# A fused encoder layer on one core: the first level of a gated scan, its parity sums moved behind its scalings

## The chip, the cores and the metric

The kernel is one program on one core of a Trainium2 chip. A core has TensorE (PE in the profile, with its weight loads as PEld), VectorE (DVE), ScalarE (ACT), GpSimd (POOL) and SyncE (SP, which only issues transfers). The profile gives each engine's instructions and what each of them waited for. The metric is the device time of one execution in microseconds (us), the median of several; less is better.

## The reference, cut to what matters

One layer over 512 tokens of width 1024, batch 1: token mixing (rotary attention with 8 query and 2 key heads of 64, beside a bidirectional gated scan, HGRN2, with 4 heads of 128 x 128), attention into 256 memory tokens, and a gated MLP with a convolution. The change lies in the gated scan:

```python
def bidirectional_gated_scan(q, logf_fwd, logf_bwd, v):
    ...
    ks = -jnp.expm1(lf)
    ...
    def step(S, xs):
        qx, kx, vx, lx = xs
        bcum = jnp.cumsum(lx, axis=-2)
        diff = bcum[..., :, None, :] - bcum[..., None, :, :]
        dec = jnp.exp(jnp.where(tri, diff, -jnp.inf))
        a = jnp.einsum("...tk,...sk,...tsk->...ts", qx, kx, dec)
        o_intra = jnp.einsum("...ts,...sv->...tv", a, vx)
        o_inter = jnp.einsum("...tk,...kv->...tv", qx * jnp.exp(bcum), S)
        ...
    return out[0] + flip(out[1])
```

For each pair of positions t and s, query and key are multiplied, weighted by all forget gates between them, and summed over the 128 channels; the two directions are added.

## The kernel before, in words

**The scan without steps.** The kernel has no loop over time. For each head, `hgrn_core(h)` builds the 512 x 512 weights between positions by levels m = 1, 2, 4, ... 256: pairs of positions whose blocks of m are neighbours are handled together. `qk` holds queries and keys of both directions with channels on the partitions and time along the row (128 x 2048); `tt` holds the products of the gates over blocks. A level does four things. ScalarE copies the keys in the level's order into a small buffer `kc` (L653). TensorE multiplies them with the queries, four matmuls of 128x128 in float32 (L656). VectorE scales both halves of `qk` by the gates (two operations of 128x512, L682), so that the next level finds them weighted, and multiplies the gates in pairs (L687). VectorE takes the level's pairs from the sums over into `diag` (L689). For m = 128 the matmuls are L663 and go to the other half of the weights; for m = 256 the keys are transposed (L668) and multiplied with the values to the state (L673, copied in L675).

**Ahead of the levels** stand the sums of position t with itself and with its neighbour (`near`, 128 x 1024: elementwise products in L634 to L639). They are split into a high part (a cast on ScalarE, L122) and a rest (a subtraction on VectorE, L123), each 128x1024, and summed over the channels by four matmuls of 128x512 against a pattern of ones and zeros, `parity` (L646); ScalarE copies the result to `diag` (L647). Behind the levels, L696 to L698 multiply the weights and the state with the values; ScalarE squares (L702), GpSimd takes the root (L297, L298), VectorE scales by root and gate (L708), TensorE turns the result (L712).

**The order.** Three cores (h = 0, 1, 2) are woven with the projections: `weave` takes the stream that is least far on by the numbers that each `yield` hands it, against totals of 100 for the projections and 53 (`CORE_SHARE`) for the cores. The first yield of a core is `PREP`. The framework then sets the final order on each engine, which is shown below. The fourth core is woven with the attention (`attention`: scores L883, turns L893) and with the projection of the memory's keys and values (L279 to L281 into `ps_b`, 128x256, results split by L122 and L123); the attention's own keys are turned there too (`turn_k`, L768, behind the second and the third projection of the memory). Other lines that come up: L318 turns the normalised memory rows, L279 to L281 are the three matmuls of every projection (high x high, high x low, low x high), L738 to L761 are the norm and rotation of the attention's queries and keys, L791 turns the queries, L223, L225 and L230 split the weights.

**Buffers.** Small buffers of 128x512 float32 come from rings: tag `th` has four, tag `ta` four, tag `tq` three; `tmp4` (128x1024) has two. A bank of the accumulators (`ps_s`, `ps_o`, `ps_c`, `ps_b`) has two per tag.

## Time and profile before

| | us |
|---|---|
| median of 3 runs | 817.83 (817.6 to 818.08) |
| the profiled execution | 818.56 |
| its span, first to last instruction | 816.8 |
| TensorE busy | 802.4 (98%) |
| VectorE busy | 583.4 (71%) |
| ScalarE busy | 481.7 (59%) |
| GpSimd busy | 137.2 (17%) |
| mean granted TensorE clock | 0.998 |

The span is from the first to the last instruction; what the profiled execution takes beyond it lies ahead of and behind the program. Rows of the timeline read: start, length (us), engine, line, operation, out<-in, shape, count, and in brackets the idle time before and what ended it. Rows of waits read: engine, what it was about to write, its line, what it waited for, total, times, longest (us). The weave of the three cores lies at 54 to 198 us, the fourth core with the attention behind it.

### The profile page before, as it was taken

What the parts mean: (1) busy time and instruction counts of PE and PEld (TensorE: products, weight loads), DVE (VectorE), ACT (ScalarE), POOL (GpSimd) and SP (SyncE); (2) the same over time, 40 slices, a digit from 0 to 9 for tenths busy, and PEclk for the clock granted to TensorE, in tenths of its full rate; (3) what the DMA queues carried; (4) which work ended last, traced back from release to release, by engine and by line L of the source; (5) the groups of instructions that cost most, each with busy time, mean ns of one, the idle gap of its engine ahead of it and who ended that gap; (6) DMA issues with size and microseconds to landing.
All of it is one profiled execution on the core that took longest, in us unless ns stands there. A gap on an engine that the chain in (4) does not pass through costs nothing.

```text
span 816.8 us, 11680 instructions
## 1 busy us (share of the span) xinstructions
PE 802.4 (98%) x4378; PEld 687.1 (84%) x4378; DVE 583.4 (71%) x875; ACT 481.7 (59%) x793; POOL 137.2 (17%) x215
## 2 busy tenths in 40 slices
PE   9999998999999999999999999999999999999996
PEld 7888877889898887888888898899999998888885
DVE  5476597659987774865453767987777788888765
ACT  5675756458988874644552543565555544566651
POOL 0111201044233201301010321211111101000301
PEclk9999999999999999999999999999999999999999
DMA  8596653558998844256734048676766577268852
GB/s 301 186 261 149 154 126 81 126 131 225 279 269 210 201 130 168 76 181 145 192 116 142 27 160 206 141 206 169 192 164 161 129 202 183 91 206 272 244 128 103
DMA packets 42458, 139.54 MB, mean 171 GB/s; under 512 B 5281, under 2 KB 6561, under 8 KB 42401
## 3 DMA queue, kind: packets, MB, share of 16 engines
q1 hardware_dynamic: 28944, 97.37, 34.9%
q0 software_dynamic: 12160, 38.54, 26.3%
q10 hardware_dynamic: 1296, 2.89, 1.0%
q8 instruction: 34, 0.56, 0.3%
q14 instruction: 24, 0.19, 0.1%
HBM read 135.11 MB, written 25.17 MB: 196 GB/s over the span
## 4 chain that ended last, share of the span: by engine, by line
PE 88%; DVE 6%; ACT 2%; DMA 2%; issue 1%; POOL 0%; DVEq 0%; POOLq 0%; SPq 0%
PE ps_b L280 9%; PE ps_b L281 9%; PE ps_b L279 9%; PE ps_s L281 6%; PE ps_s L280 6%; PE ps_s L279 6%; PE ps_o L279 5%; PE ps_o L281 5%; PE ps_o L280 5%; PE ps_c L279 5%; PE ps_c L280 5%; PE ps_c L281 5%; PE ps_c L656 3%; PE ps_o L904 2%; DMA raw<-in_w_dram 2%; PE ps_s L883 2%
## 5 line engine op out<-in xcount | busy, mean ns | idle before, releaser
L223 ACT CAST wh<-raw 128x1024 fp32r<-128x1024 f32 x110 | 113.7, 1035 | 106.8 <-PE ps_b L280 27.8
L225 DVE TENSOR_TENSOR wl<-raw,wh 128x1024 fp32r<-128x1024 f32 (+1 forms) x77 | 92.2, 1199 | 72.3 <-ACT wh L223 72.2
L279 PE MATMUL ps_b<-big,wh 128*128 128x512 f32 (+1 forms) x344 | 122.2, 355 | 0.0
L281 PE MATMUL ps_b<-big,wl 128*128 128x512 f32 (+1 forms) x344 | 120.9, 352 | 0.0
L280 PE MATMUL ps_b<-big,wh 128*128 128x512 f32 (+1 forms) x344 | 120.7, 351 | 0.0
L281 PEld LDWEIGHTS ps_b<-big,wl 128*128 128x128 f32 x344 | 65.0, 189 | 8.5 <-DMA wl<-in_wu_dram 0.2
L279 PEld LDWEIGHTS ps_b<-big,wh 128*128 128x128 f32 x344 | 65.1, 189 | 8.2
L280 PEld LDWEIGHTS ps_b<-big,wh 128*128 128x128 f32 x344 | 65.1, 189 | 8.2
L682 DVE TENSOR_TENSOR big<-big 128x512 f32<-128x512 f32 x64 | 48.1, 761 | 10.4 <-PE ps_c L656 6.2
L279 PE MATMUL ps_s<-wh,big 128*128 128x512 f32 (+1 forms) x140 | 53.2, 381 | 0.9 <-DVE big L123 0.9
L280 PE MATMUL ps_s<-wl,big 128*128 128x512 f32 (+1 forms) x140 | 53.2, 380 | 0.0
L281 PE MATMUL ps_s<-wh,big 128*128 128x512 f32 (+1 forms) x140 | 52.8, 377 | 0.0
L231 POOL DMA_DIRECT2D wl<-in_w_dram x33 | 29.5, 894 | 119.4 <-ACT wl L230 94.9
L123 DVE TENSOR_TENSOR big<-ps_o,big 128x512 fp32r<-128x512 f32 x54 | 36.9, 686 | 12.2 <-ACT big L122 11.9
L122 ACT CAST big<-ps_o 128x512 fp32r<-128x512 f32 x54 | 31.7, 589 | 16.1 <-PE ps_o L1007 7.5
L279 PE MATMUL ps_s<-big,wh 128*128 128x256 f32 (+1 forms) x120 | 40.0, 333 | 0.0
L280 PE MATMUL ps_s<-big,wh 128*128 128x256 f32 (+1 forms) x120 | 39.9, 333 | 0.0
L281 PE MATMUL ps_s<-big,wl 128*128 128x256 f32 (+1 forms) x120 | 39.9, 332 | 0.0
L280 PE MATMUL ps_c<-big,wh 128*128 128x256 f32 (+1 forms) x120 | 39.1, 326 | 0.0
L279 PE MATMUL ps_c<-big,wh 128*128 128x256 f32 (+1 forms) x120 | 39.1, 325 | 0.0
L281 PE MATMUL ps_c<-big,wl 128*128 128x256 f32 (+1 forms) x120 | 39.0, 325 | 0.0
L279 PE MATMUL ps_o<-wh,big 128*128 128x512 f32 (+1 forms) x102 | 38.9, 381 | 0.0
(316 smaller groups left out, 2150.4 us busy)
## 6 DMA issues: line engine op xcount, KB each, us to landing
raw<-in_w_dram SPq DMA_DIRECT2D x91, 512.0 KB, 3.5
wl<-in_w_dram POOLq DMA_DIRECT2D x33, 512.0 KB, 7.5
sum_t<-in_wd_dram SPq DMA_DIRECT2D x20, 512.0 KB, 6.1
tmp<-in_wu_dram SPq DMA_DIRECT2D x14, 512.0 KB, 8.0
sum_t<-in_wd_dram POOLq DMA_DIRECT2D x10, 512.0 KB, 8.3
sum_t<-sum_t POOLq DMA_DIRECT2D x10, 512.0 KB, 7.9
big<-sum_t SPq DMA_DIRECT2D x10, 512.0 KB, 4.5
raw<-sum_t SPq DMA_DIRECT2D x10, 512.0 KB, 3.9
```

The lines of the kernel that those rows point to most:

```text
L122: nc.scalar.copy(hi, src)
L123: (eng or nc.vector).tensor_sub(lo, src, hi.bitcast(F32))
L223: nc.scalar.copy(wh, raw)
L225: last_low[0] = nc.vector.tensor_sub(wl[:, :by_dma], raw[:, :by_dma], wh[:, :by_dma].bitcast(F32)).ins
L231: nc.gpsimd.dma_start(wl[:, by_dma:], source(i)[:, by_dma:], accum_op=ALU.add)
L279: nc.tensor.matmul(o, a[0], b[0], start=start, stop=False, skip_group_check=again)
L280: nc.tensor.matmul(o, a[0], b[1], start=False, stop=False, skip_group_check=again)
L281: last_mm[0] = nc.tensor.matmul(o, a[1], b[0], start=False, stop=stop, skip_group_check=again).ins
L656: nc.tensor.matmul(o[:, b, :], kc[:, blk(b)], pat(qk, b * P, [[2 * m, P // (2 * m)], [T + m, 2], [1, m]]), start=True, stop=True)
L682: nc.vector.tensor_tensor(out=c, in0=c, in1=pat(tt, toff + off, [[2, npair], [gap, 2], [0, m]]), op=ALU.mult)
L883: nc.tensor.matmul(s, qT[h // 4][:, h % 4, blk(qb)], kT[:, 2 * (h // 4) + c, :], start=c == 0, stop=c == 1)
L904: nc.tensor.matmul(o, vv[:, c, h // 4].rearrange("p a d -> p (a d)"), pt[j][:, c, :], start=c + j == 0, stop=c == 3 and j == 1)
```

## The change

Three edits. In `hgrn_core` the products `near` are no longer split in two operations into two `tmp4` buffers, but by halves: two casts and two subtractions of 128x512 into four buffers of the ring `th`, which the sum of the keys and the level copies use too. The four sums and the copy into `diag` move from ahead of the levels into level m = 1, behind its scalings (L676 in the new numbering) and the product of its gates (L681); the yield `PREP` stands in front of them and grows from 1.5 to 2.0. The pattern `parity` is written behind the warming matmuls instead of ahead of them. In the new numbering the sums are L691, the level's matmul L650, its scalings L676.

```diff
-PREP = 1.5
+PREP = 2.0
...
     nc.gpsimd.memset(ones, 1.0)
-    for i in range(2):
-        nc.gpsimd.memset(parity.rearrange("p (i two) -> p i two", two=2)[:, :, i].bitcast(F32), 1.0 - i)
     nc.vector.memset(warm[:, :256], 0.0)
...
     hT = new_act()
+    for i in range(2):
+        nc.gpsimd.memset(parity.rearrange("p (i two) -> p i two", two=2)[:, :, i].bitcast(F32), 1.0 - i)
...
-        hi, lo = [tmp4([P, 2, T], F32R) for _ in range(2)]
-        split(hi, lo, near.rearrange("p (a t) -> p a t", a=2))
-        yield PREP
-        o = bank("c")
+        sides = [[tmp2(dt=F32R, tag="th") for _ in range(2)] for _ in range(2)]
         for i in range(2):
-            for part in (hi, lo):
-                nc.tensor.matmul(o, parity[:, i:i + P], part[:, i], start=i == 0 and part is hi, stop=i == 1 and part is lo)
-        nc.scalar.copy(diag, o.rearrange("p (b n) -> p b n", b=NB))
-        yield 1.0
+            split(*sides[i], near[:, i * T:i * T + T])
         toff = 0
...
-            if m > 1:
-                yield 1.0
+            if m == 1:
+                yield PREP
+                o = bank("c")
+                for n in range(2):
+                    for k in range(2):
+                        nc.tensor.matmul(o, parity[:, n:n + P], sides[n][k], start=n + k == 0, stop=n + k == 2)
+                nc.scalar.copy(diag, o.rearrange("p (b n) -> p b n", b=NB))
+            yield 1.0
```

On TensorE at the end of core 1 (about 126 to 132 us): L696 to L698 are the core's product with the values, L712 its turn, L318 the memory's turns, L279 the query projection's first matmul. Before:

```order
L696 MATMUL ps_c<-big 128x128
L697 MATMUL ps_c<-big 128x128
L698 MATMUL ps_c<-big 128x128
L281 MATMUL ps_b<-big,wl 128x512
L318 MATMUL ps_s<-ident,big 128x128 x4
L318 MATMUL ps_o<-ident,big 128x128 x4
L318 MATMUL ps_s<-ident,big 128x128 x4
L318 MATMUL ps_o<-ident,big 128x128 x4
L712 MATMUL ps_c<-ident,tmp_1088 128x128 x4
L279 MATMUL ps_s<-wh,big 128x512
```

And now, where L662 and L667 are the transposed keys and the state of the same core (L668 and L673 before):

```order
L662 MATMUL ps_c<-ident,big 128x128 x4
L318 MATMUL ps_s<-ident,big 128x128 x4
L318 MATMUL ps_o<-ident,big 128x128 x4
L667 MATMUL ps_c<-big 128x128 x4
L696 MATMUL ps_c<-big 128x128
L697 MATMUL ps_c<-big 128x128
L318 MATMUL ps_s<-ident,big 128x128 x4
L318 MATMUL ps_o<-ident,big 128x128 x2
L698 MATMUL ps_c<-big 128x128
...
L318 MATMUL ps_o<-ident,big 128x128 x2
L279 MATMUL ps_s<-wh,big 128x512
```

The memory's turns stand between the core's last matmuls, and L712 stands 18 matmuls further on.

On VectorE at the same place: L708 scales the core's output, L123 splits the memory's turns, L611 and L581 belong to the projections of head 3, L726 and L728 build the rotation tables. Before:

```order
L611 SCALAR_TENSOR_TENSOR big<-big,oml,tmp_875 128x512
L581 TENSOR_TENSOR tmp_1109<-ps_b,big 128x512
L708 SCALAR_TENSOR_TENSOR tmp_1088<-ps_c,small,big 128x128 x4
L611 SCALAR_TENSOR_TENSOR big<-big,oml,tmp_875 128x512
L123 TENSOR_TENSOR big<-ps_s,big 128x4x128
L123 TENSOR_TENSOR big<-ps_o,big 128x4x128
```

And now (L681 is the product of gates in the next core):

```order
L611 SCALAR_TENSOR_TENSOR big<-big,oml,tmp_879 128x512
L681 TENSOR_TENSOR big<-big 128x512
L123 TENSOR_TENSOR big<-ps_s,big 128x4x128
L123 TENSOR_TENSOR big<-ps_o,big 128x4x128
L123 TENSOR_TENSOR big<-ps_s,big 128x4x128
L726 TENSOR_TENSOR big<-big,qkg 128x256
...
L123 TENSOR_TENSOR big<-ps_o,big 128x4x128
L708 SCALAR_TENSOR_TENSOR tmp_1102<-ps_c,small,big 128x128 x4
```

The four splits of the memory stood behind L708 and stand ahead of it.

On TensorE where the attention's keys are turned (203 to 210 us): the sums of the fourth core (L646, now L691), the turns (L768), and the memory's projection (L279 to L281 into `ps_b`). Before:

```order
L281 MATMUL ps_b<-big,wl 128x256
L768 MATMUL ps_s<-ident_r,big 128x128 x8
L646 MATMUL ps_c<-tmp_1846,parity 128x512
L768 MATMUL ps_o<-ident_r,big 128x128
L279 MATMUL ps_b<-big,wh 128x256
...
L646 MATMUL ps_c<-tmp_1847,parity 128x512
L646 MATMUL ps_c<-tmp_1846,parity 128x512
L646 MATMUL ps_c<-tmp_1847,parity 128x512
...
L768 MATMUL ps_o<-ident_r,big 128x128 x7
```

And now:

```order
L768 MATMUL ps_s<-ident_r,big 128x128 x8
L691 MATMUL ps_c<-tmp_1858,parity 128x512
L768 MATMUL ps_o<-ident_r,big 128x128
L691 MATMUL ps_c<-tmp_1859,parity 128x512
L691 MATMUL ps_c<-tmp_1860,parity 128x512
L768 MATMUL ps_o<-ident_r,big 128x128 x3
L691 MATMUL ps_c<-tmp_1861,parity 128x512
L768 MATMUL ps_o<-ident_r,big 128x128 x4
L279 MATMUL ps_b<-big,wh 128x256
```

The 24 matmuls of the memory's projection that stood between the turns stand behind them. Ahead of the turns there are 48 of them in both orders.

## The prediction

> **What bounds the kernel now.** I read the page's first part, then its chain of waits, then busy time in stretches of 20 us, then TensorE's waits by line. First part, and the chain's shares:

> ```profile
> PE 802.4 (98%) x4378; PEld 687.1 (84%) x4378; DVE 583.4 (71%) x875; ACT 481.7 (59%) x793; POOL 137.2 (17%) x215
> ...
> PE 88%; DVE 6%; ACT 2%; DMA 2%; issue 1%; POOL 0%; DVEq 0%; POOLq 0%; SPq 0%
> ```

> TensorE is busy 802.4 of 816.8 us, and the change takes no matmul away. So at most the 14.4 us in which it stands can be won, and only those near moved instructions. The stretches (from:to, length, busy us by engine, granted clock, DMA share, GB/s) tell where it stands:

> ```profile
> 100.00:120.00 20.00, 19.14 (x108) 15.41 (x107) 19.57 (x34) 10.07 (x14) 2.57 (x3) 1.00 0.66 144
> 120.00:140.00 20.00, 17.44 (x101) 14.20 (x100) 13.83 (x24) 14.69 (x32) 2.15 (x3) 1.00 0.29 68
> 180.00:200.00 20.00, 19.39 (x161) 18.37 (x160) 19.14 (x38) 16.69 (x29) 8.36 (x10) 1.00 0.87 233
> 200.00:220.00 20.00, 18.57 (x142) 17.01 (x140) 18.50 (x47) 18.37 (x33) 6.40 (x10) 1.00 1.03 280
> 220.00:240.00 20.00, 20.00 (x147) 18.52 (x147) 17.86 (x39) 17.97 (x39) 6.04 (x6) 1.00 0.98 262
> ```

> The order of instructions differs only between about 54 and 316 us. There TensorE loses 0.86, 2.56, 0.61 and 1.43 us in the first four stretches. From 180 to 240 VectorE (third busy figure) is nearly full, ScalarE (fourth) too from 200: there TensorE has little lead. TensorE's waits by line (total, times, longest):

> ```profile
> PE ps_c L712 <- DVE tmp L708: 1.1, 1, 1.1
> PE ps_c L646 <- ACT tmp L122: 1.0, 2, 0.5
> PE ps_s L279 <- DVE big L123: 0.9, 1, 0.9
> PE ps_c L656 <- DVE big L687: 0.9, 2, 0.6
> PE ps_c L646 <- DVE tmp L123: 0.7, 2, 0.5
> PE ps_c L791 <- DVE tmp L123: 0.6, 1, 0.6
> ```

> The first level's sums (L646) cost 1.7 us of waiting in all. The change moves them, but also what is woven around them.

> **Part 1, the smaller split.** One cast and one subtraction of 128x1024 become two of 128x512 each. The rows: the old prices (first two), the two sums of core 2, and the new prices, from splits of that size elsewhere (last two):

> ```profile
> 105.32 1.19 DVE L123 TENSOR_TENSOR tmp<-big,tmp 128x1024 fp32r<-128x1024 f32 x1
> 138.63 1.05 ACT L122 CAST tmp<-big 128x1024 fp32r<-128x1024 f32 x1 [0.56 <-DVE big L639]
> 139.73 0.50 PE L646 MATMUL ps_c<-tmp,parity 128*128 128x512 f32 x1 [0.49 <-ACT tmp L122]
> 141.30 0.96 PE L646 MATMUL ps_c<-tmp,parity 128*128 128x512 f32 x3 [0.16 <-DVE tmp L123]
> 189.42 0.62 ACT L122 CAST tmp<-tmp 128x512 fp32r<-128x512 f32 x1 [0.25 <-DVE tmp L749]
> 190.51 0.68 DVE L123 TENSOR_TENSOR tmp<-tmp,tmp 128x512 fp32r<-128x512 f32 x1
> ```

> Per head ScalarE gets 2 x 0.62 - 1.05 = 0.19 us more work and VectorE 2 x 0.68 - 1.19 = 0.17. TensorE's first sum can start half a cast earlier, about 0.43. The four halves take the buffers that the level copies (L653) rotate through, so the copies for the second and third level wait until a sum has been done. Who is late then is a level (L656), for which TensorE has waited 0.6 at the longest by the rows above: bounds 0 and 3 x 0.6 for the three cores that run here, and I take 0.25 for each, 0.8.

> **Part 2, the sums behind the scalings.** In core 2 (the last rows above) TensorE stood 0.49 + 0.16 by the rows, and counted from start to start it lost about 1.2 (a matmul that starts after a pause takes 0.50, a running one 0.40). In the new order eight matmuls of other work (0.23 each from start to start, 1.8 us) stand ahead of the sums that did not before: gain 1.0 (bounds 0 and 1.2). In core 1 VectorE is busy 19.57 of 20 in that stretch, so the low halves and the scalings cannot come sooner; the 1.7 us lost there from start to start shrink only to 1.5: gain 0.2 (bounds -0.5 and 1.2). In core 0 no wait is shown before, and its second level comes about 2 us later under projection matmuls: nothing (bounds -0.3 and 0).

> **Part 3, the end of core 1.** The larger PREP hands 0.5 more per head to the other stream, so later pieces slip against each other. Before, the four turns of the memory (L318), the turn of core 1's output (L712) and the query projection (L279), which writes the bank ps_s that the turns used, stood in a row:

> ```profile
> 127.56 0.60 PE L318 MATMUL ps_o<-ident,big 128*128 128x128 f32 x4
> 127.73 1.04 POOL L298 TENSOR_TENSOR small<-small,nhalf 128x4 f32<-128x4 f32 x1
> 128.80 1.13 DVE L708 SCALAR_TENSOR_TENSOR tmp<-ps_c,small,big 128x128 f32<-128x128 f32 x4 [1.66 <-POOL small L298]
> 129.30 1.01 PE L712 MATMUL ps_c<-ident,tmp 128*128 128x128 f32 x4 [1.14 <-DVE tmp L708]
> 130.50 0.68 DVE L123 TENSOR_TENSOR big<-ps_s,big 128x512 fp32r<-128x512 f32 x1
> 131.24 0.50 PE L279 MATMUL ps_s<-wh,big 128*128 128x512 f32 x1 [0.93 <-DVE big L123]
> ```

> Four turns take 0.44 (0.11 each, as in L318's rows of four), so L712 could have started at 128.0 and did at 129.30; L279 could have at 129.74 and did at 131.24: 1.3 + 1.5 = 2.8 us. The splits of the memory (L123) were queued on VectorE behind L708, which waited for the root on GpSimd (L298). In the new order the memory's turns stand around the state's matmuls, their splits come ahead of L708, and L712 comes 18 matmuls after the projection's first. L708 still waits for the root, but nobody that TensorE needs at once is queued behind it. New are two small waits of about 0.15, where the transposes of the keys and the state's matmuls have less between them. Gain 2.5 (bounds 1.3, if the splits are still late, and 2.8).

> **Part 4, the query turns.** L708 of core 2 held VectorE's queue until 172.85, and the rope work of the queries behind it was late for their turn (L791):

> ```profile
> 169.84 0.39 PE L698 MATMUL ps_c<-big 128*128 128x128 f32 x2
> ...
> 172.85 0.35 DVE L708 SCALAR_TENSOR_TENSOR tmp<-ps_c,small,big 128x128 f32<-128x128 f32 x1 [11.05 <-POOL small L298]
> ...
> 181.30 0.85 PE L791 MATMUL ps_c<-ident_r,tmp 128*128 128x128 f32 x8 [0.61 <-DVE tmp L123]
> ```

> Now the rope work of two blocks stands ahead of L708: gain 0.7 (bounds 0 and 0.75). Sum of parts 2 to 4: 1.0 + 0.2 + 2.5 + 0.7 = 4.4, less the 0.8 of part 1: **3.6 us ahead** when the key and value projection ends (198.04 before, 194.4 now).

> **Part 5, the key turns, where I expect it to go.** The rows behind that point:

> ```profile
> 197.11 0.27 DVE L738 TENSOR_REDUCE small<-tmp 128x2 f32<-128x128 f32 x1
> 198.04 0.28 PE L279 MATMUL ps_b<-big,wh 128*128 128x256 f32 x1
> 203.80 1.08 PE L768 MATMUL ps_s<-ident_r,big 128*128 128x128 f32 x8
> 209.01 0.42 DVE L761 TENSOR_TENSOR big<-tmp,big 128x256 fp32r<-128x256 f32 x1
> 213.13 0.63 PE L883 MATMUL ps_s<-big 128*128 128x512 f32 x2
> ```

> L738 is the first step of the key's norm and L761 (the row at 209.01) the last of its four blocks, 209.43 - 197.11 = 12.3 us of a chain through VectorE, ScalarE and GpSimd. Before, TensorE had 48 matmuls (198.04 to 203.80, 0.12 each), then turns with 24 more matmuls between them, and came to the last turns when L761 was just done. In the new order the core's sums and all sixteen key turns stand behind the 48 with nothing between. And VectorE isn't 3.6 us ahead: core 2's attention product (L696 to L698) stands behind two query turns now, its last at about 178.3 by the matmuls ahead of it, so L708 comes 3.0 us later (as 169.84 to 172.85) at 181.3. From there 16 operations of 128x512 at 0.60 from start to start (9.6), three like L611 (2.0) and nine small ones (2.5), 14.1 us without a gap, stand ahead of the first key reduction; with about 0.9 of waits for ScalarE's copies it is at 196.3, **0.8 us earlier, not 3.6**. The chain, from which one split of 0.41 has moved away, ends at 196.3 + 11.9 = 208.2. TensorE arrives at 194.4 + 5.8, does 2.5 us of turns and sums as they are released, and stands until 208.2, some 5.5 us in pieces. From there the last turns (0.5), 36 matmuls (4.3), a level (0.9) and four scores (0.9) end at 214.8; before, the same work less one level of 0.94 ended at 215.56 (the row below), so at 214.6. The 3.6 us are gone, and 0.2 more: a loss of 3.8 (bounds 0, if VectorE keeps up, and 5.5). Behind that point ScalarE has two level copies (L653) more done, 1.2 us, but TensorE is busy 20.00 of 20 from 220 to 240, so there is little to win: gain 0.3 (bounds 0 and 1.2).

> ```profile
> 214.09 1.16 PE L656 MATMUL ps_c<-big,tmp 128*128 128x128 f32 x8 [0.33 <-ACT tmp L653]
> 215.56 0.28 PE L279 MATMUL ps_b<-big,wh 128*128 128x256 f32 x1
> ```

> **Part 6, the pattern written later.** It is first read at about 56 us, and TensorE's first matmul also waits for a fill on VectorE that ends with the old order's on GpSimd: nothing (bounds 0 and 0.1 gained).

> Sum: -3.6 + 3.8 - 0.3 = -0.1 us. Against the profiled execution, 816.8 of span and 1.76 around it, that is 818.5; the median of the runs shown is 0.73 lower, so **817.7**. Two tenths of a per cent, 1.6 us, is about what can be told from no change.

> **Rivals.** *B, the gain stays.* If the key chain moves up with TensorE, because VectorE's queue has slack that its row sum of 14.1 us doesn't show or L708 comes sooner, part 5 is 0: 817.83 - 3.6 = 814.2. For it: 19.39 of 20 on TensorE and 11.05 us of idle VectorE before L708, room to work ahead. Against: 19.14 busy of 20 on VectorE from 180.

> *C, the pause lowers the clock.* Slower. In the trace pauses up to 1.3 us leave the granted clock at 1.00, but after the empty start matmuls ran at another pace:

> ```profile
> 6.73 0.63 PE L510 MATMUL ps_o<-wh,big 128*128 128x512 f32 x1
> 7.15 0.49 PE L510 MATMUL ps_s<-wl,big 128*128 128x512 f32 x1
> ...
> 7.72 0.40 PE L510 MATMUL ps_s<-wl,big 128*128 128x512 f32 x1
> 7.95 0.40 PE L510 MATMUL ps_o<-wl,big 128*128 128x512 f32 x1
> ```

> 0.42 between starts up to 7.15, 0.23 from then on. If part 5's pause of 5.5 us has the same effect for a stretch as long as the first one (1.3 to 7.2), the half pace costs half of 5.9: 2.9 us, 817.7 + 2.9 = 820.6. It decides once TensorE has nothing at all for long enough, between 1.3 and 5.5 us. Against: the pause comes in pieces with turns in between. [...]

> *D, nothing moves*: parts 2 to 4 gain less than 1 and TensorE doesn't arrive early, so that part 5 loses as little: 817.8, counted with the forecast.

> **How the numbers follow.** Forecast with D 0.46 (its own range 816.0 to 819.4), B 0.35 (813.2 to 816.0), C 0.19 (819.2 to 821.2). 813.8 to 820.4 leaves out a fifth of B and half of C, under 2 in 10. Faster than 816.2: B and a little of the forecast's lower end, 0.37; slower than 819.5: C's greater part and the forecast's upper end, 0.19; within, 0.44.

> **What would show it.** Right: no wait of L712 for L708 near 127 us and none of L279 for L123; sums of core 2 without a wait; the first key reduction near 196; a wait of the L768 turns for L761 of several us near 203 to 208. Wrong: that wait below 2 us (then B), a granted clock under 1.00 from 200 to 220 (C), or TensorE's busy time from 120 to 140 still near 17.4 (D).

## The result

The changed kernel takes **821.52 us** (821.02 to 823.82, 5 runs) against 817.83 (817.60 to 818.14) of the kernel before: a ratio of **1.0049**, interval 1.0035 to 1.0064. It is slower by 3.7 us, outside the stated range of 813.8 to 820.4, and on the side that was given a chance of 0.19. The profiled execution took 823.82 us with a span of 822.0.

Two later comparisons, each with its own runs of the kernel before beside it (which spread more there, 817.38 to 823.09), gave 1.0014 (1.0000 to 1.0028) and 1.0034 (1.0019 to 1.0048). So the change makes the kernel slower by something between 1 and 4 us. In what follows kernels are compared by the ratio within their own comparison, and traces stretch by stretch.

### The profile page after: what moved, and what is told of

It is laid out like the page before. It is cut to its first block, busy times and chain, and to the rows that moved or that the text cites. A ratio compares the mean times of both kernels' runs of the same rounds, so it can differ in the third digit from the quotient of the medians.

```text
span 822.0 us, 11679 instructions
## 1 busy us (share of the span) xinstructions
PE 805.7 (98%) x4378; PEld 690.6 (84%) x4378; DVE 583.9 (71%) x879; ACT 482.9 (59%) x797; POOL 136.3 (17%) x215
## 5 line engine op out<-in xcount | busy, mean ns | idle before, releaser
L223 ACT CAST wh<-raw 128x1024 fp32r<-128x1024 f32 x110 | 113.8, 1036 | 114.3 <-PE ps_b L280 28.6
L279 PE MATMUL ps_b<-big,wh 128*128 128x512 f32 (+1 forms) x344 | 123.1, 358 | 0.0
L281 PE MATMUL ps_b<-big,wl 128*128 128x512 f32 (+1 forms) x344 | 121.6, 354 | 0.2 <-DMA wl<-in_wu_dram 0.2
L280 PE MATMUL ps_b<-big,wh 128*128 128x512 f32 (+1 forms) x344 | 121.5, 353 | 0.0
L281 PEld LDWEIGHTS ps_b<-big,wl 128*128 128x128 f32 x344 | 65.8, 191 | 8.8 <-DMA wl<-in_wu_dram 0.4
L280 PEld LDWEIGHTS ps_b<-big,wh 128*128 128x128 f32 x344 | 65.9, 192 | 8.2
L279 PEld LDWEIGHTS ps_b<-big,wh 128*128 128x128 f32 x344 | 65.9, 192 | 8.1
L676 DVE TENSOR_TENSOR big<-big 128x512 f32<-128x512 f32 x64 | 47.2, 745 | 17.9 <-PE ps_c L650 9.1
L280 PE MATMUL ps_s<-wl,big 128*128 128x512 f32 (+1 forms) x140 | 53.2, 380 | 0.0
L279 PE MATMUL ps_s<-wh,big 128*128 128x512 f32 (+1 forms) x140 | 53.2, 381 | 0.0
L281 PE MATMUL ps_s<-wh,big 128*128 128x512 f32 (+1 forms) x140 | 53.0, 378 | 0.0
L123 DVE TENSOR_TENSOR big<-ps_o,big 128x512 fp32r<-128x512 f32 x54 | 37.1, 687 | 14.3 <-ACT big L122 12.3
L122 ACT CAST big<-ps_o 128x512 fp32r<-128x512 f32 x54 | 31.8, 590 | 18.7 <-PE ps_o L1007 7.5
L279 PE MATMUL ps_s<-big,wh 128*128 128x256 f32 (+1 forms) x120 | 40.0, 333 | 0.0
L280 PE MATMUL ps_s<-big,wh 128*128 128x256 f32 (+1 forms) x120 | 39.9, 333 | 0.0
L281 PE MATMUL ps_s<-big,wl 128*128 128x256 f32 (+1 forms) x120 | 39.9, 332 | 0.0
L280 PE MATMUL ps_c<-big,wh 128*128 128x256 f32 (+1 forms) x120 | 39.1, 325 | 0.0
L279 PE MATMUL ps_c<-big,wh 128*128 128x256 f32 (+1 forms) x120 | 39.0, 325 | 0.0
L281 PE MATMUL ps_c<-big,wl 128*128 128x256 f32 (+1 forms) x120 | 39.0, 325 | 0.0
L279 PE MATMUL ps_o<-wh,big 128*128 128x512 f32 (+1 forms) x102 | 38.8, 380 | 0.0
```

The lines of the kernel that those rows point to most:

```text
L122: nc.scalar.copy(hi, src)
L123: (eng or nc.vector).tensor_sub(lo, src, hi.bitcast(F32))
L223: nc.scalar.copy(wh, raw)
L279: nc.tensor.matmul(o, a[0], b[0], start=start, stop=False, skip_group_check=again)
L280: nc.tensor.matmul(o, a[0], b[1], start=False, stop=False, skip_group_check=again)
L281: last_mm[0] = nc.tensor.matmul(o, a[1], b[0], start=False, stop=stop, skip_group_check=again).ins
```

## The profile after

The stretches that answer to those of before (from:to, length, busy us of PE, PEld, DVE, ACT and POOL, granted clock, DMA share, GB/s):

```profile
100.00:120.00 20.00, 18.84 (x105) 15.29 (x103) 19.38 (x35) 12.55 (x18) 2.60 (x3) 1.00 0.68 152
120.00:140.00 20.00, 20.00 (x120) 16.89 (x119) 16.67 (x32) 14.06 (x31) 3.04 (x4) 1.00 0.37 92
180.00:200.00 20.00, 19.66 (x163) 18.89 (x162) 17.80 (x42) 16.25 (x34) 8.84 (x11) 1.00 0.74 181
200.00:220.00 20.00, 16.52 (x97) 14.72 (x97) 15.80 (x37) 14.78 (x26) 6.44 (x10) 0.74 0.86 241
```

From 120 to 140 TensorE no longer stands (20.00, before 17.44): the end of core 1 is repaired as forecast. From 200 to 220 it is busy 16.52 instead of 18.57, and the figure behind the five engines is new: the granted clock is **0.74**. TensorE's waits by line say where:

```profile
PE ps_c L691 <- DVE tmp L123: 1.7, 2, 1.1
...
PE ps_c L650 <- ACT tmp L647: 1.2, 1, 1.2
PE ps_s L768 <- DVE big L761: 0.9, 1, 0.9
PE ps_o L768 <- DVE big L761: 0.9, 1, 0.9
PE ps_s L768 <- ACT big L759: 0.7, 1, 0.7
...
PE ps_o L768 <- ACT big L759: 0.5, 1, 0.5
PE ps_o L768 <- DVE big L759: 0.5, 1, 0.5
```

The waits of L712 for L708, of L279 for L123 and of L791 are gone from the list. In their place stand the five waits of the key turns (L768), 3.5 us, one after the other, as released by the four blocks of the key's norm, and one wait of a level (L650) in core 0. The first level's sums (L691) still cost 1.7, as much as L646 before. The timeline of TensorE through the key turns (start, length):

```profile
201.75 0.46 PE L768 MATMUL ps_s<-ident_r,big 128*128 128x128 f32 x4
202.91 0.28 PE L768 MATMUL ps_s<-ident_r,big 128*128 128x128 f32 x1 [0.70 <-ACT big L759]
204.11 0.45 PE L768 MATMUL ps_s<-ident_r,big 128*128 128x128 f32 x3 [0.92 <-DVE big L761]
...
209.47 0.63 PE L768 MATMUL ps_o<-ident_r,big 128*128 128x128 f32 x3 [0.87 <-DVE big L761]
209.89 0.54 PE L279 MATMUL ps_b<-big,wh 128*128 128x256 f32 x1
...
212.58 0.41 PE L279 MATMUL ps_b<-big,wh 128*128 128x256 f32 x1
212.79 0.41 PE L280 MATMUL ps_b<-big,wh 128*128 128x256 f32 x1
...
215.87 0.28 PE L279 MATMUL ps_b<-big,wh 128*128 128x256 f32 x1
215.99 0.28 PE L280 MATMUL ps_b<-big,wh 128*128 128x256 f32 x1
```

The pause ends at 209.47, but the matmuls behind it start 0.21 us apart (212.58 to 212.79) until 215.4, and 0.12 apart from there on (215.87 to 215.99). Nothing waits in those rows: TensorE itself runs at about half pace. One-us stretches around both edges (columns as above):

```profile
205.00:206.00 1.00, 0.46 (x3) 0.44 (x2) 1.00 (x4) 1.00 (x4) 0.53 (x1) 0.60 1.03 270
206.00:207.00 1.00, 1.00 (x5) 0.74 (x4) 1.00 (x4) 0.95 (x2) 0.00 (x0) 0.50 1.05 287
...
214.00:215.00 1.00, 1.00 (x7) 1.00 (x6) 0.00 (x0) 0.09 (x1) 0.00 (x0) 0.50 1.10 227
215.00:216.00 1.00, 1.00 (x9) 1.00 (x9) 0.28 (x1) 0.00 (x0) 0.00 (x0) 0.78 0.63 123
216.00:217.00 1.00, 1.00 (x11) 1.00 (x10) 1.00 (x3) 0.57 (x2) 0.00 (x0) 1.00 0.07 12
```

Away from the edges the clock is 1.00 or 0.50 in these rows. A mean of 0.60 over a us says that it fell 0.2 us into it, at 205.2 (stretches of 0.1 us show 1.00 up to 205.2 and 0.52 and 0.50 behind it); 0.78 says that it came back at 215.44. That is 10.2 us. It was rival C, at its place: with the pauses at the key turns the clock went down, to 0.50. Rival C's condition, that TensorE has nothing at all for long enough, between 1.3 and 5.5 us, was an estimate, and the clock fell without it: the longest single wait there is 0.92 us.

## The experiments

**What they had to tell apart.** Theory: the pauses at the key turns are made by the order (no other matmuls stand between the turns), and they take the clock down. Rivals: the four small buffers hold up the levels; the later sums do; the larger PREP does; or the fall of the clock costs nothing because TensorE waits anyway. They came in three comparisons (e1 to e4, e5 to e8, e9 to e12), each on another chip, and the table gives them in that order.

| kernel | edit | us (median) | ratio to before | interval | clock 200-220 | clock down from, for us |
|---|---|---|---|---|---|---|
| e1_fill | change, 9 idle matmuls at the turns | 820.18 | 1.0010 | 0.9996 to 1.0023 | 0.83 | 206.9, 6.8 |
| e2_prep15 | change, PREP 1.5 | 818.66 | 0.9996 | 0.9984 to 1.0008 | 0.91 | 207.1, 3.4 |
| e3_split | before, split by halves only | 816.75 | 0.9965 | 0.9948 to 0.9982 | 1.00 | never |
| e4_move | change, large split buffers | 819.50 | 1.0003 | 0.9990 to 1.0016 | 0.74 | 202.5, 10.2 |
| e5_change | the change | 820.87 | 1.0014 | 1.0000 to 1.0028 | 0.83 | 204.6, 6.8 |
| e6_fill12 | change, 12 larger idle matmuls | 818.10 | 0.9984 | 0.9975 to 0.9993 | 1.00 | never |
| e7_prep20 | before, PREP 2.0 only | 817.61 | 0.9975 | 0.9965 to 0.9984 | 0.83 | 203.5, 6.8 |
| e8_split_share50 | before, split, CORE_SHARE 50 | 817.18 | 0.9962 | 0.9948 to 0.9976 | 0.91 | 203.5, 3.4 |
| e9_change_again | the change | 822.46 | 1.0034 | 1.0019 to 1.0048 | 0.83 | 207.0, 6.8 |
| e10_split_prep20 | before, split and PREP 2.0 | 819.30 | 0.9989 | 0.9976 to 1.0002 | 0.83 | 203.9, 6.8 |
| e11_split_share51 | before, split, CORE_SHARE 51 | 815.48 | 0.9953 | 0.9937 to 0.9969 | 1.00 | never |
| e12_split_share58 | before, split, CORE_SHARE 58 | 815.81 | 0.9950 | 0.9937 to 0.9963 | 1.00 | never |

The last column is worked out from one-us stretches of each trace as above. The medians of before in the three comparisons are 819.66, 819.89 and 820.15.

**Idle work in the pause (e1, e6).** `turn_k` puts matmuls into the bank of its turns, which then overwrite them, for the blocks 1 to 3: three of 256 columns each in e1 (shown), four of 512 columns in e6:

```diff
+        for i in range(FILL if b else 0):
+            nc.tensor.matmul(o.rearrange("p k n -> p (k n)")[:, 0:256], kv["m"].get(0, slice(0, P))[0],
+                             kv["m"].get(0, slice(0, M))[0], start=True, stop=True)
         for i in range(4):
             nc.tensor.transpose(o[:, i, :].bitcast(F32R), kd4[:, i, :], ident_r)
```

> The changed kernel with nine matmuls of 128x256 more, whose results are overwritten: three into the bank of each of the key-turn blocks 1, 2 and 3, ahead of the turns (9 x 0.12 = 1.1 us of work, put where TensorE stands). The order of all other instructions on TensorE around the turns is that of the changed kernel. Theory (the pauses at the key turns halve the clock): the granted clock stays 1.00 from 204 to 216, the 24 following matmuls run at 0.12 again, and the time falls by the 2.9 us of half pace, to about 818.6. Rival (the clock falls for another reason, or its fall costs nothing because TensorE waits anyway): 821.5, up to 822.6 if the added work is paid.

> The changed kernel with twelve idle matmuls of 128x512 (12 x 0.23 = 2.7 us), four ahead of each of the key-turn blocks 1, 2 and 3; their results are overwritten. With them the order puts 24 matmuls of the memory's projection ahead of the last three turns. Theory: TensorE is busy enough through the turns, the granted clock stays 1.00, and although 2.7 us of work are added the time falls by 2 to 4 us against the changed kernel. Rival (the pause doesn't set the clock): the clock falls as before, the time rises by up to 2.7.

e1 missed: 1.1 us of idle work was too little, and the clock fell all the same, at 206.9. Its comparison holds no run of the change, whose ratios elsewhere are 1.0014 to 1.0049, so its 1.0010 doesn't tell what the idle work was worth. e6 hit. The 20-us stretch of e1, of e6, and of the change in e6's comparison, one row from each:

```profile
200.00:220.00 20.00, 17.08 (x106) 15.26 (x106) 15.68 (x36) 14.69 (x26) 5.03 (x8) 0.83 0.83 232
```

```profile
200.00:220.00 20.00, 18.03 (x128) 16.07 (x127) 17.03 (x43) 16.34 (x29) 5.53 (x8) 1.00 0.97 262
```

```profile
200.00:220.00 20.00, 16.35 (x102) 14.33 (x101) 16.16 (x37) 15.80 (x29) 4.84 (x8) 0.83 0.93 255
```

With 2.7 us of useless work more, e6 is 2.8 us faster than the change in the same comparison (818.10 to 820.87). The clock stays 1.00. This is not the clock alone: in e6's order 24 matmuls of the memory's projection come ahead of the last three turns, as the expectation says, and shorten the last pause. No run holds the clock and keeps the change's order exactly, so the two are not separated by a run. The half pace of e5 is worth 1.4 us (worked out below), so the 2.8 are not the clock's alone.

**Part by part (e2, e3, e4, e7, e10).**

```diff
 e2: change, PREP = 1.5      e7: before, PREP = 2.0
 e3: before, with
-        hi, lo = [tmp4([P, 2, T], F32R) for _ in range(2)]
-        split(hi, lo, near.rearrange("p (a t) -> p a t", a=2))
+        sides = [[tmp2(dt=F32R, tag="th") for _ in range(2)] for _ in range(2)]
+        for i in range(2):
+            split(*sides[i], near[:, i * T:i * T + T])
 e4: the change with the two removed lines in place of the added ones
 e10: e3, PREP = 2.0
```

> The changed kernel with PREP back at 1.5. The order at the key turns and at the end of core 1 stays that of the change. Theory: pauses and half clock are there as well, 821.5 within 1. Rival (the larger PREP is what costs, by handing out the wrong work): 818 or less.

> The kernel before with one edit: the split of the first level by halves into four small buffers; the sums stay ahead of the scalings and PREP stays 1.5. The order at the end of core 1 is already that of the change, and 24 matmuls stand ahead of the last four key turns. Theory: the gain at the end of core 1 (2.7) is there, the pause at the key turns is shorter by about the last piece (0.9), the clock stays 1.00: 815.5. Rival (the four small buffers, which the level copies need too, are what costs): a level waits about 1.3 us in core 0 and the time is 819 or more.

> The changed kernel, but the first level is split into the two large buffers as before; the sums stand behind the scalings and PREP is 2.0. 24 matmuls stand ahead of the last three key turns. Theory: no wait of a level copy for a buffer in core 0 (1.3 us less), the gain at the end of core 1 is there, the clock stays 1.00: 815.5. Rival (the sums behind the scalings are what costs): 820 to 821.5 with a clock of 1.00.

> The kernel before with PREP at 2.0 and nothing else. The order at the end of core 1 has L712 behind the projection's first matmuls as in the change, and 24 matmuls stand ahead of the last four key turns. Theory: gain at the end of core 1 (2.7), a pause at the key turns like that of the split alone, clock 1.00: 0.2 to 0.4% faster than before. Rival (PREP is what makes the pause): clock at 0.50 for 3 to 10 us, same or slower than before.

> The change without its move: the split by halves and PREP 2.0, the sums ahead of the scalings. 24 matmuls of the memory's projection stand ahead of the last four key turns, where the changed kernel has none. Theory: a shorter pause, the clock at 1.00 or down for one stretch of 3.4 us, 0.2 to 0.4% faster than before. Rival (PREP 2.0 and the split together make the pause, the move is free): as the changed kernel.

Each of the first two parts alone makes the kernel *faster*: the split by 0.35% (e3), PREP by 0.25% (e7). Together they are no better than before (0.9989), and the move on top of them makes it slower: 822.46 us (e9) against 819.30 (e10) in one comparison. With PREP at 1.5 the move costs as much: 818.66 (e2) against 816.75 (e3). The rival of e3 is out for e3: the small buffers cost nothing that shows in its time, and no level waits in its core 0. In other traces with these buffers one does, as shown below. The rival of e2 was half right: with PREP at 1.5 the changed kernel is as fast as before, its clock down for 3.4 us and not 6.8 to 10.2. e2's theory (821.5) missed. So did e4 in both its readings: it has no buffers to wait for and the clock is down for 10.2 us all the same, at the time of before. My expectation of e7 (clock 1.00) was wrong, and still it is faster; e10 came between its two. The rows of e3 and of e7:

```profile
200.00:220.00 20.00, 18.17 (x130) 15.76 (x129) 16.73 (x42) 16.68 (x30) 4.71 (x7) 1.00 1.05 302
```

```profile
200.00:220.00 20.00, 17.42 (x109) 15.61 (x108) 15.94 (x38) 15.40 (x29) 4.88 (x8) 0.83 1.00 270
```

All five kernels gain about the same ahead of this stage: the memory's projection, which starts at 198.04 before, starts at 193.4 to 195.4 in them. What tells them apart is what happens from 200 to 220.

**That stage in every trace.** Count each matmul of a trace by the step from its start to the next one's start in a row without pauses at full clock, as the trace of before shows it: 0.227 us for 512 columns, 0.120 for 256, 0.11 for 128; the turns by `ident_r`, which start 0.06 to 0.09 apart there, are put at 0.064. This gives how much earlier than in the kernel before TensorE has started the same amount of work, its lead (idle matmuls aren't counted as work done). Between what the kernel before does at 198 and at 220 us, the lead falls by 5.7 us in the first profile and 6.1 in e4 (10.2 us at half clock each); by 3.5 (e10), 3.9 (e7), 4.7 (e5), 4.8 (e9) and 5.7 (e1) with 6.8 us at half clock; by 3.1 (e2) and 1.7 (e8) with 3.4. With the clock up it falls by 1.4 in e3 and by 3.1 in e6, 2.7 of them idle matmuls, and rises by 1.4 in e11 and 1.2 in e12. Pauses and half pace are in these figures together.

**The change again (e5, e9).**

> The changed kernel itself again, beside the others of this call. Theory: pause at the key turns, granted clock at 0.50 for about 10 us from 205, time 0.3 to 0.6% above the kernel before; without the late weight load in core 0 (1.4 us at 59) that the first profile shows. Rival (that late load belongs to the change, because the level copies wait for the new small buffers): the wait at 59 us is there again.

> The changed kernel a third time, beside the next three. Theory: clock at 0.50 for a multiple of 3.4 us at the key turns, 0.1 to 0.5% slower than before. Rival (the slower time of the first comparison was that chip's): within 0.1% of before or faster, with the same trace.

The pause and the fall of the clock are in each of the three traces of the change, at 204.6 to 207.0. The wait of the level in core 0 is in two of them. ScalarE's rows there, of the kernel before, of the change, and of e5:

```profile
56.26 0.69 ACT L653 COPY tmp<-big 128x512 f32<-128x512 f32 x1
...
57.80 1.03 ACT L223 CAST wh<-raw 128x1024 fp32r<-128x1024 f32 x1
```

```profile
59.05 1.05 ACT L223 CAST wh<-raw 128x1024 fp32r<-128x1024 f32 x1 [1.88 <-PE ps_c L691]
60.00 0.66 ACT L647 COPY tmp<-big 128x512 f32<-128x512 f32 x1
```

```profile
57.05 1.05 ACT L223 CAST wh<-raw 128x1024 fp32r<-128x1024 f32 x1 [0.21 <-DMA raw<-in_w_dram]
```

Before, the copy of the level's keys (L653) stands ahead of a weight cast (L223). With the four small buffers it has to wait for a sum, and stands behind the cast (L647 in the new numbering). The cast waits for its weights; where they come late, as in the first profile and in e9, the level is late by 1.2 to 1.6 us, and where they come in time, as in e5, by nothing. The first profile names TensorE's sums as what ended the cast's wait, the rows of e5 and e9 name the load (in e9 the cast starts at 59.34 after waiting 2.22 us for it). Both parts of my expectation and of its rival were too simple: how late the load comes differs from run to run of the same kernel, and the order that exposes the level to it is the change's. The time of e5 (0.14% above before) missed its range of 0.3 to 0.6%; that of e9 hit.

**Work between the turns (e8, e11, e12).** The edit is that of e8; e11 has 51.0 and e12 58.0:

```diff
 e3, and
-CORE_SHARE, ATT_LEAD = 53.0, 4.0
+CORE_SHARE, ATT_LEAD = 50.0, 4.0
```

> The kernel before with the split by halves alone (sums ahead of the scalings, PREP 1.5) and CORE_SHARE 50 for 53. The order puts matmuls of the memory's projection between the sums of the fourth core and between the key turns. Theory: no pause over 0.6 us from 200 to 220, clock 1.00, 0.4 to 0.7% faster than before. Rival (the key chain on VectorE sets the end of this stage whatever stands between): as the split alone, 0.35% faster.

> The kernel before with the split by halves and CORE_SHARE 51. The order spreads 30 matmuls of the memory's projection over the key turns and the core's sums in six places. Theory: no pause over 0.6 us from 200 to 220, clock 1.00, 0.4 to 0.6% faster than before. Rival (the key chain on VectorE sets the end of the stage anyway): 0.35% as the split alone.

> The kernel before with the split by halves and CORE_SHARE 58. The first two sums come ahead of the turns and 24 matmuls of the memory's projection stand between the first and the last turns. Theory: pauses like the kernel before, clock 1.00, 0.3 to 0.5% faster than before. Rival: a pause elsewhere, since the cores end earlier, same as before.

e11 and e12 hit: the order spreads the memory's matmuls over the turns, the clock stays up, and both are **0.5% faster than the kernel before** (0.9953 and 0.9950), the lowest ratios of the table, though e3's interval overlaps theirs. The stretch of e11, and three of its rows at the turns:

```profile
200.00:220.00 20.00, 19.60 (x147) 18.11 (x146) 18.68 (x47) 19.36 (x38) 4.90 (x7) 1.00 0.99 273
```

```profile
206.27 0.75 PE L769 MATMUL ps_o<-ident_r,big 128*128 128x128 f32 x5
206.86 0.35 PE L279 MATMUL ps_b<-big,wh 128*128 128x256 f32 x1
...
208.00 0.28 PE L769 MATMUL ps_o<-ident_r,big 128*128 128x128 f32 x1 [0.20 <-DVE big L762]
```

TensorE is busy 19.60 of 20 there, a us more than before, and the longest wait of a turn is 0.20. The same key chain, for which TensorE's turns waited 3.5 us in the change, costs it nearly nothing when other work stands between. e8 was expected to have no pause either; it had one of 0.9 near 203, its clock fell for 3.4 us, its trace holds a late load in core 0 as well (1.5 us at its level), and it stayed at the split's level, as its rival said.

## Why the prediction was wrong

**Parts 2 to 4, the gain ahead of the key turns: right in sum, in part by luck.** Forecast 3.6 us, to 194.4. In e5, where no load is late:

```profile
194.23 0.28 PE L279 MATMUL ps_b<-big,wh 128*128 128x256 f32 x1
```

198.04 - 194.23 = 3.8. But 0.5 of the 3.8 stood ahead of the weave already: core 0's first cast (L122) starts at 54.75 in e5 and at 55.23 before. Counted by the lead, the end of core 1 brought 2.7, close to the 2.5 worked out: in the first profile TensorE's work from 120 to 140 is 2.56 us more, and 1.14 + 0.93 of it are the waits of L712 and L279 that are gone. The other 0.49 is a wait of core 2's sums, and there one of 0.6 stayed (the smaller of the two for L123 above), behind 140; these sums brought 0.3 and not 1.0, and the query turns 0.1 and not 0.7. Against these two, the loss of part 1 was mis-sized the other way. I put it at 0.25 for each core; it is nothing in a run in which the weights come in time, and 1.2 to 1.6 in core 0 where they don't, so that in the first profile the projection starts at 195.99.

**Part 5, the pause: right, step by step, in e5.** Forecast, and e5: L708 at 181.3, and 180.84; the first key reduction (L738) at 196.3, and 196.03; the end of the last L761 at 208.2, and 207.66; work goes on at 208.7, and at 208.13:

```profile
180.84 0.35 DVE L708 SCALAR_TENSOR_TENSOR tmp<-ps_c,small,big 128x128 f32<-128x128 f32 x1 [1.17 <-POOL small L298]
...
196.03 0.28 DVE L738 TENSOR_REDUCE small<-tmp 128x2 f32<-128x128 f32 x1 [0.41 <-ACT tmp L736]
...
207.26 0.40 DVE L761 TENSOR_TENSOR big<-tmp,big 128x256 fp32r<-128x256 f32 x1
```

A gain that runs into a chain on another engine ended there, as forecast, and rival B (the gain stays) is out. In the first profile the delay of core 0 is carried along on VectorE: that reduction starts at 197.79, and the last L761 ends at 209.42.

**The step that failed is the half pace, which the sum of the forecast puts at nothing.** I gave rival C 0.19 and counted against it that the pause comes in pieces with turns in between. That is no argument: in the 3.4 us ahead of the fall TensorE was busy 1.58 us in the first profile and 1.94 in e5, and the clock fell. The trace of before had shown as much, which the prediction overlooked: at its end the clock is 0.50 from 812.9 on, and in the 3.41 us ahead of that TensorE was busy 0.45. The price was right in kind. In the first profile the half pace lasts from the end of the pause (209.9) to 215.44. A step of 256 columns there takes 0.21 instead of 0.12, so 0.44 of that time is lost, 2.4 us (rival C: 2.9, by taking half); in e5, from 208.1 to 211.4, it is 1.4. Less 2.4, the first result would be 819.1, inside the forecast's own range of 816.0 to 819.4; that is worked out from the trace, not run. Every stretch at half clock in the table is 3.4, 6.8 or 10.2 us long.

**Part 5's tail.** Forecast 0.3 gained behind the key turns. In the first profile and in e5 TensorE waits instead 0.6 and 0.7 near 350 us (L318 behind L311), in a part of the program whose order the change doesn't touch; e9 shows 0.2. From turn to turn (starts of L318 at 341.98 and 349.38 in e5, 340.82 and 347.15 before) e5 loses 1.1 there. With that e5's account closes: 3.8 us ahead, 4.7 lost from 198 to 220 (1.4 by half pace, so 3.3 by the pause, forecast 3.8), 1.1 here and 0.2 elsewhere make 2.2, as the spans do (819.0 against 816.8). The wait near 350 lies behind a weight load that is late in e5. Why the load is late was not tried and stays open.

**Parts 1 (its prices) and 6.** In core 0 of the first profile the casts take 0.62 and 0.60, the subtractions 0.68 and 0.69, as taken. The warming matmuls start at 1.27 with `parity` early or late; no run has that edit alone.

## What to carry to other kernels

## What the runs showed that I had not expected

At the key turns the granted clock fell without an idle stretch. TensorE's busy time in the 3.4 us ahead of the fall, in the nine traces where it fell: 1.39 (e7), 1.40 (e2), 1.58 (the first profile), 1.60 (e4), 1.78 (e10), 1.94 (e5), 2.03 (e9), 2.14 (e8) and 2.37 us (e1). In the five traces in which it stayed up, the emptiest 3.4 us between 199 and 212 held 2.29 (e6), 2.5 (e12), 2.75 (e3), 2.85 (before) and 3.2 (e11). Busy time sets no limit, then: e6 and e1 overlap, and elsewhere the clock stayed up over less (e8, 56.77 to 60.18, with 1.98). Busy time also counts a matmul of 256 columns that stands alone with 0.28 us, where in a row one starts every 0.12 (L279 and L280 at 215.87 and 215.99 in the first profile).

Counted by their steps as above, the matmuls that start in the 3.41 us ahead of the fall come to 0.68 us in the first profile, to 0.94 in e5, and to 0.23 ahead of 812.9 in the trace of before. That sets no limit either: in the trace of before those in the 3.41 us from 127.78 on come to 0.55 (TensorE is busy 1.33 of the 3.40 us from 128.00 on), and the clock stayed at 1.00. In the first profile the clock falls at 205.20, comes back at 215.44 and falls again at 819.60, near the end: 10.24 and 604.16 us, 3 and 177 times 3.413. What decides the fall these runs do not show; no run was made to test it.

Three groups of four idle matmuls, 2.7 us of work whose result is thrown away, made the changed kernel 2.8 us faster (with the reordering that they brought).
